# Seven block products in place of eight for 18 of the 22 input tiles of a last projection

## The chip, the cores and the metric

The kernel runs on one core of a Trainium2 chip. A core has a matrix engine (TensorE, PE in the profile), three engines for elementwise work (VectorE or DVE, ScalarE or ACT, GpSimd or POOL), a queue engine (SyncE, SP) that issues most transfers, and 16 DMA engines. The on-chip memory SBUF and the accumulators PSUM (eight banks of 128 x 512 floats) have 128 partitions; HBM is the memory outside. The metric is the time of one execution on the device in microseconds. Of several runs the median is given.

## The reference

One layer of a diffusion backbone over 512 latent tokens of width 1024, with 256 context tokens: a token mixer, then a gated MLP with a 3x3 depthwise convolution on its gate branch, and a final RMSNorm. The change lies in the second half:

```python
h = modulate(rms_norm(x_lat, norm2_g), sh2, sc2)
x_lat = x_lat + gt2 * conv_ffn(h, w_up, conv_w, conv_b, w_down)
return rms_norm(x_lat, final_g)

def conv_ffn(h, w_up, conv_w, conv_b, w_down, rows, cols):
    val, gate = jnp.split(h @ w_up, 2, axis=-1)
    gate = depthwise_conv_grid(gate, conv_w, conv_b, rows, cols)
    return (jax.nn.gelu(gate, approximate=False) * val) @ w_down
```

The inner width is 2816, that is 22 tiles of 128 channels. `x_lat` at this point, after the token mixer, is called x2 in the kernel.

## The kernel before

**Products.** Every product is made in three matmuls (`mm3`): both factors are split into a high part (a cast to the fp32r type, by ScalarE) and a low part (the difference, a subtraction by GpSimd or, where the call says `V`, by VectorE), and high x high, high x low and low x high are added up in PSUM. `split` is that pair of operations; `split_w` does it for a 128 x 1024 weight tile, into a ring of four pairs (`whl`, tags whi and wlo). Weight tiles arrive through a ring of three raw tiles (`raw_tile`). A further ring, `S4`, has 30 tiles of 128 x 1024 for everything that lives longer.

**Up projection.** It runs over the 22 channel tiles. For tile i, `up_weights` loads two weight tiles (gate and value), `up_mm` makes 48 matmuls into two PSUM banks (tag pb, four banks, so two tiles of them), and `up_out` finishes: ScalarE starts the convolution with the middle tap, VectorE adds the other eight taps, reading PSUM, ScalarE applies the Gelu, VectorE multiplies by the value branch, and `split` by ScalarE and VectorE leaves the tile of hidden values (128 channels x 512 tokens, high and low) in `hid[i]`, one S4 tile. The first three tiles overlap the norm before them. In four of the tiles (4, 8, 12, 16) VectorE also works out a quarter of the gate vector gt2 (`mod_part`, with two loads of 512 KB), which `mod_bcast` adds to the broadcast tile `gt2` one tile later.

**Last projection.** The hidden tiles are the stationary factor, in blocks of 128 tokens, and `w_down`'s rows the moving one, 512 columns at a time. All of the output, four token blocks by two halves, stands in the eight PSUM banks (`acc`). For each of the first 18 input tiles, `load_down` loads 512 KB of w_down, VectorE multiplies it by gt2, `split_w` splits it with ScalarE and GpSimd, and `down` makes 4 x 2 x 3 = 24 matmuls. The last NL = 4 input tiles are loaded and split ahead (`wl_`, in S4 tiles) and are done block by block of tokens at the end, so that one block's residual add, norm and store run beside the products of the next. x2 stands in four SBUF tiles (pool emf) from the norm to the end.

**Order.** The program is written as one sequence; a planner orders each engine's instructions by a simulated timeline, with the sequence as priority, and places buffers from the free ones of a ring. `tc.issue_after(x)` holds an instruction back until x is issued. Each engine then runs its own list in order. SP issues almost all loads in such a list, and waits in it for buffers to come free.

Helpers that record most operations have one line each, so nearly all groups of the profile carry L88 or L87, and tiles tell them apart: ac is the convolution, raw a loaded weight tile, whi and wlo its parts, s any S4 tile, pb and p the PSUM tiles of one and two banks, x the tiles of x2.

Of the kernel before, what the change touches and what calls it, by code (L numbers as in the profile page):

```python
# [9 lines left out]
F32 = mybir.dt.float32  # L10
# [3 lines left out]
ALU = mybir.AluOpType  # L14
# [7 lines left out]
GH = 4  # L22
FF = 2816
NF = FF // 128
EPS = 1e-6
ATT_SCALE = 96.0 ** -0.5
GQ_SCALE = 128.0 ** -0.5
# [43 lines left out]
def block_kernel(ctx: ExitStack, tc: tile.TileContext, p, out):  # L71
# [43 lines left out]
    def S4(shape, dt=F32R):  # L115
        return tl(s4, shape, dt, "s4")
# [16 lines left out]
    def tt(eng, out_, a, b, op):  # L133
        return eng.tensor_tensor(out=out_, in0=a, in1=b, op=op)
# [153 lines left out]
    def mp_tile():  # L288
        return sm(256, "mp", 2)
# [1032 lines left out]
    behind.clear()  # L1322


    emf = ctx.enter_context(tc.tile_pool(name="emf", bufs=1))
# [23 lines left out]
    with tc.tile_pool(name="emg", bufs=1) as em_:  # L1349
# [52 lines left out]
        def w_out_norm(t):  # L1402
            cs = slice(t * 128, (t + 1) * 128)
            mp = p2()
            for k in range(8):
                for half in range(2):
                    hs = slice(half * 512, (half + 1) * 512)
                    mm3(mp[:, hs], mg[k][:, 0, cs], mg[k][:, 1, cs], wo[k][0][:, hs], wo[k][1][:, hs], k == 0, k == 7)
            xn = mraw()
            for half in range(2):  # L1410
                hs = slice(half * 512, (half + 1) * 512)
                tt(V, xn[:, hs], mp[:, hs], gt1[:, hs], ALU.mult)
                tt(V, x2[t][:, hs], x2[t][:, hs], xn[:, hs], ALU.add)
# [43 lines left out]
            up_mm(w0[i], ps0[i], 256, 512)  # L1457


    with tc.tile_pool(name="eff", bufs=1) as ef:  # L1460
        fg = tl(ef, [128, 1024], F32, "fg")
        gt2 = tl(ef, [128, 1024], F32, "gt2")
        G.dma_start(out=gt2, in_=p["b_ada"][0:1, 5120:6144].broadcast_to([128, 1024]))
        G.dma_start(out=fg, in_=p["final_g"].rearrange("(a b) -> a b", a=1).broadcast_to([128, 1024]))
        hid, gelu = [], []

        def up_out(i, ps):
            gp, vp = ps
            ac = tl(ef, [128, 512], F32, "ac", 2)

            def cw(dy, dx):
                n = ((dy + 1) * 3 + dx + 1) * NF + i
                return cwT[:, n:n + 1]

            A.activation(ac, gp, AF.Identity, scale=cw(0, 0), bias=col("conv_b", i))
            g3 = gp.rearrange("p (r c) -> p r c", c=64)
            a3 = ac.rearrange("p (r c) -> p r c", c=64)
# [12 lines left out]
            hid.append(hd)  # L1490

        for i in range(3):
            up_out(i, ps0[i])
        for i in range(3, NF):
            w = up_weights(i)
            if i in (4, 8, 12, 16):
                part = mod_part(5120 + (i - 4) * 64, mp_tile(), raw_tile)
            ps = (pb(), pb())
            up_mm(w, ps, 0, 512)
            up_out(i, ps)  # L1500

            if i in (5, 9, 13, 17):
                mod_bcast(part, gt2[:, (i - 5) * 64:(i - 1) * 64])

        acc = []
        for t in range(4):
            if t < 2:
                z = p2()
                acc.append([z[:, 0:512], z[:, 512:1024]])
            else:  # L1510
                acc.append([pb(), pb()])

        def down(k, t, half, w, a=0, n=512):
            cs, hs = slice(t * 128, (t + 1) * 128), slice(half * 512 + a, half * 512 + a + n)
            mm3(acc[t][half][:, a:a + n], hid[k][:, 0, cs], hid[k][:, 1, cs], w[0][:, hs], w[1][:, hs], k == 0,
                k == NF - 1)

        def load_down(k):

            r = raw_tile()  # L1520
            SY.dma_start(out=r, in_=w_down[:, k, :])
            tt(V, r, r, gt2, ALU.mult)
            return r

        NL = 4
# [3 lines left out]
        for k in range(NF - NL):  # L1529
            if k in (8, 10, 12, 14):  # L1530
                r = load_down(NF - NL + k // 2 - 4)
                wl_.append((S4([128, 1024]), S4([128, 1024])))
                split(*wl_[-1], r)
            w = split_w(load_down(k))
            for t in range(4):
                for half in range(2):
                    down(k, t, half, w)

        def residual(t, a, b, ps):
            tt(V, x2[t][:, a:b], x2[t][:, a:b], ps, ALU.add)  # L1540

        for t in range(4):
            last = t == 3
            o_t = tl(ef, [128, 1024], F32, "ot", 2)
# [76 lines left out]
```

## Time and profile before

| | |
|---|---|
| median of 3 runs | 895.43 us (895.09 to 897.04) |
| profiled execution | 894.83 us, its span 893.0 us |
| granted TensorE clock | 0.999 |
| HBM read, written | 97.78 MB, 2.10 MB |
| busy in the span: POOL | 372.5 us |
| loads of w_down | 22 of 512 KB, 3.6 us each to landing |

The span goes from the first to the last instruction. A line of the profile's groups gives line, engine, operation, output and inputs, shape, count, busy time, mean of one in ns, and the idle time in front of it with what ended it. A line of the chain gives start, length, and the work that the end of the kernel waited for then. Matmuls overlap one another, so the length of a chain piece divided by its matmuls, not the duration of a single one, is the time that each takes.

### The profile page before, as it was taken

Reading aid. Unit: us, or ns where it says so; the run is one execution under the profiler, and the core shown is the slowest. Engines: PE = TensorE matmul, PEld = TensorE weight load, DVE = VectorE, ACT = ScalarE, POOL = GpSimd, SP = SyncE. Lnnn points to the kernel's source line nnn. Section 1 sums busy time; section 2 is a strip of 40 time slices with the busy share of each in tenths; the row PEclk is TensorE's granted clock in tenths of the full one; section 3 lists DMA queues with packets and bytes.
Section 4 is the critical chain, followed back from the end, with each engine's and each line's share of the span. In section 5 each row is a group of like instructions: output and inputs, shape, how many; then the busy total and the mean of one; then the engine's idle time right before and its main releaser. Section 6 shows DMA issues by size and latency. Waiting matters only on the chain.

```text
span 893.0 us, 12644 instructions
## 1 busy us (share of the span) xinstructions
PE 878.4 (98%) x4852; PEld 748.1 (84%) x4852; DVE 608.2 (68%) x993; ACT 391.8 (44%) x648; POOL 372.5 (42%) x221
## 2 busy tenths in 40 slices
PE   7999999999999999999999999999999999999996
PEld 5788899888888888888888899888888888888885
DVE  5487788876978686845763775987778778744404
ACT  4365676763463636334554332443333333322204
POOL 2512364460624343433754324344444444356704
PEclk9999999999999999999999999999999999999999
DMA  9960001225414241437963314425343433244202
GB/s 293 319 175 1 1 5 33 72 72 165 106 48 134 52 135 51 119 89 249 274 209 95 95 48 138 122 72 143 96 139 110 131 114 95 70 142 142 71 0 95
DMA packets 131564, 100.89 MB, mean 113 GB/s; under 512 B 6826, under 2 KB 121874, under 8 KB 131504
## 3 DMA queue, kind: packets, MB, share of 16 engines
q1 hardware_dynamic: 130560, 98.09, 37.6%
q0 software_dynamic: 688, 1.70, 0.5%
q8 instruction: 38, 0.62, 0.3%
q10 hardware_dynamic: 256, 0.30, 0.1%
q14 instruction: 22, 0.18, 0.1%
HBM read 97.78 MB, written 2.10 MB: 112 GB/s over the span
## 4 chain that ended last, share of the span: by engine, by line
PE 92%; DVE 3%; DMA 2%; ACT 2%; issue 1%; POOL 0%; SPq 0%; DVEq 0%; ACTq 0%; POOLq 0%
PE pb L88 49%; PE p L88 23%; PE pb L87 14%; PE p L87 6%; DMA raw<-in_w_ada_dram 2%; DVE s L88 1%; ACT P L88 1%; DVE mx L88 0%; DVE kT L88 0%; ACT ph L88 0%; DVE P L88 0%; ACT kT L88 0%; ACT s L88 0%; DVE X L88 0%; DVE pl L88 0%
## 5 line engine op out<-in xcount | busy, mean ns | idle before, releaser
L88 POOL TENSOR_TENSOR wlo<-raw,whi 128x1024 fp32r<-128x1024 f32 (+1 forms) x106 | 242.8, 2298 | 322.1 <-ACT whi L88 291.5
L88 PE MATMUL pb<-s,whi 128*128 128x512 f32 (+1 forms) x906 | 272.2, 383 | 0.0
L88 PEld LDWEIGHTS pb<-s,whi 128*128 128x128 f32 x906 | 167.4, 188 | 32.1
L88 PE MATMUL pb<-s,wlo 128*128 128x512 f32 (+1 forms) x453 | 172.9, 382 | 0.0
L88 ACT CAST whi<-raw 128x1024 fp32r<-128x1024 f32 (+1 forms) x106 | 103.1, 975 | 142.3 <-issue 60.1
L88 DVE SCALAR_TENSOR_TENSOR ac<-pb,cwT,ac 128x441 f32<-128x441 f32 (+2 forms) x160 | 110.8, 693 | 12.3 <-ACT ac L88 8.6
L87 PE MATMUL pb<-s,whi 128*128 128x512 f32 x320 | 101.2, 394 | 0.0
L88 PEld LDWEIGHTS pb<-s,wlo 128*128 128x128 f32 x453 | 85.2, 188 | 16.4
L88 PE MATMUL p<-s,s 128*128 128x512 f32 (+1 forms) x392 | 81.9, 364 | 0.6 <-DVE s L88 0.5
L88 PEld LDWEIGHTS p<-s,s 128*128 128x128 f32 x392 | 65.9, 189 | 12.5 <-DVE s L88 1.1
L88 PE MATMUL p<-whi,s 128*128 128x512 f32 x208 | 69.2, 393 | 0.0
L87 PEld LDWEIGHTS pb<-s,whi 128*128 128x128 f32 x320 | 59.3, 188 | 11.5
L88 DVE TENSOR_TENSOR raw<-raw,gt 128x1024 f32<-128x1024 f32 x22 | 39.2, 1783 | 35.6 <-DMA raw<-in_w_down_dram 35.6
L87 PE MATMUL pb<-s,wlo 128*128 128x512 f32 x160 | 62.8, 393 | 0.0
L88 PE MATMUL pb<-whi,s 128*128 128x512 f32 x176 | 57.7, 390 | 0.0
L88 ACT ACTIVATE ac<-ac 128x512 f32<-128x512 f32 x22 | 13.9, 632 | 80.0 <-DVE ac L88 80.0
L88 PEld LDWEIGHTS p<-whi,s 128*128 128x128 f32 x208 | 39.1, 188 | 8.2 <-ACT s L88 0.3
L88 POOL TENSOR_TENSOR s<-raw,s 128x1024 fp32r<-128x1024 f32 (+1 forms) x10 | 24.5, 2461 | 43.2 <-ACT s L88 43.2
L88 PE MATMUL pb<-s,s 128*32 128x128 f32 (+2 forms) x322 | 41.4, 315 | 0.9 <-DMA s<-in_w_ada_dram 0.9
L88 PE MATMUL p<-kT,s 128*128 128x512 f32 (+1 forms) x192 | 41.2, 351 | 0.9 <-ACT P L88 0.9
L88 DVE TENSOR_TENSOR pl<-pb,ph 128x512 fp32r<-128x512 f32 x48 | 32.9, 686 | 13.0 <-ACT ph L88 12.5
L88 PE MATMUL p<-wlo,s 128*128 128x512 f32 x104 | 40.5, 390 | 0.0
(252 smaller groups left out, 1554.4 us busy)
## 6 DMA issues: line engine op xcount, KB each, us to landing
raw<-in_w_up_dram SPq DMA_DIRECT2D x44, 512.0 KB, 3.9
raw<-in_w_in_dram SPq DMA_DIRECT2D x28, 512.0 KB, 4.1
raw<-in_w_down_dram SPq DMA_DIRECT2D x22, 512.0 KB, 3.6
s<-in_w_ada_dram SPq DMA_DIRECT2D x20, 512.0 KB, 6.3
raw<-in_w_ada_dram SPq DMA_DIRECT2D x18, 512.0 KB, 4.4
xn<-in_w_ada_dram SPq DMA_DIRECT2D x10, 512.0 KB, 4.9
kT<-in_w_in_dram SPq DMA_DIRECT2D x8, 320.0 KB, 7.7
s<-in_x_dram SPq DMA_DIRECT2D x4, 512.0 KB, 5.0
```

The source lines that it names most:

```text
L87: return fn(*args, **kw)
L88: ins = fn(*args, **kw)
```

## The change

Channel tiles are taken in pairs (NP = 9 pairs, tiles 0 to 17). Tokens are halved (256 each) and output columns are halved (512 each), so that a pair is a product of 2 x 2 blocks: A11, A12 (first token half; even and odd tile), A21, A22 (second half), times B11, B12 (columns of the even tile's rows of w_down) and B21, B22 (of the odd tile's). Eight block products become seven (Winograd's form), with sums of the factors: S1 = A21 + A22, S2 = S1 - A11, S3 = A11 - A21, S4 = A12 - S2; T1 = B12 - B11, T2 = B22 - T1, T3 = B22 - B12, T4 = B21 - T2. The sum over the nine pairs is made in PSUM for each of the seven products, and the products are combined once.

- `up_out` for tiles below 18 writes A-blocks and their sums to `edge` (A11, S1, S3, S2, A21) and `second` (A12, S4, A22) by VectorE; `edge`'s first four are split into the S4 tiles `first`, `second` is kept unsplit.
- `weight_sums(n)`, in up tiles 6, 8, ..., 20 and 21, loads the pair's two tiles of w_down into a ring of two (`rawd`), VectorE makes T1 and T3, GpSimd T2 and T4, and SP stores both tiles to HBM (`sums_`).
- In the last projection a first loop over the pairs makes the four products p1 = A11 B11, p6 = S2 T2, p7 = S3 T3, p5 = S1 T1 in all eight banks, with weights from w_down and from `sums_`; they are combined into u1, u2, u7, c22 in SBUF; a second loop makes p2 = A12 B21, p4 = A22 T4, p3 = S4 B22. Their splits are by VectorE.
- The weights of these 18 tiles aren't multiplied by gt2 any more; `gated` multiplies the combined output by it and adds x2. The last four tiles stay as they were, with PSUM begun afresh.
- x2 is stored to HBM by ACT's queue after the norm and loaded again in the last projection; its SBUF goes to `second` and gt2. gt2's and final_g's loads move from POOL's queue to SP's. The parts of gt2 are made in tiles 6, 10, 14, 18. The descriptor scratch of DMAs issued by GpSimd is 4096 bytes.
- One add of 256 columns goes from the last token block.

```diff
+NP = (NF - NL) // 2
+SUM_AT = [6, 8, 10, 12, 14, 16, 18, 20, 21]
...
+    x2_ = [tl(hbm, [128, 1024], F32, f"x2_{t}") for t in range(4)]
+    sums_ = [tl(hbm, [128, 2048], F32, f"ws_{i}") for i in range(NP)]
...
             A.activation(xn, x2[t], AF.Square, accum_out=s2)
+            A.dma_start(out=x2_[t], in_=x2[t])
             r2 = rstd_exp(s2, 1, 1.0 / D)
...
+    emf_.__exit__(None, None, None)
+    kept = ctx.enter_context(tc.tile_pool(name="kept", bufs=1))
+    gt2 = tl(kept, [128, 1024], F32, "gt2")
+    SY.dma_start(out=gt2, in_=p["b_ada"][0:1, 5120:6144].broadcast_to([128, 1024]))
...
-            tt(V, ac, vp, ac, ALU.mult)
-            hd = S4([128, 2, 512])
-            split(hd[:, 0, :], hd[:, 1, :], ac, V)
-            hid.append(hd)
+            if i >= 2 * NP:
+                tt(V, ac, vp, ac, ALU.mult)
+                hid[i] = S4([128, 2, 512])
+                split(hid[i][:, 0, :], hid[i][:, 1, :], ac, V)
+            elif i % 2 == 0:
+                edge[0] = tl(ef, [128, 1280], F32, "edge", 1)
+                z = grp(edge[0], 5)
+                tt(V, z[:, 0::4, :], grp(vp, 2), grp(ac, 2), ALU.mult)
+                sub(V, z[:, 2, :], z[:, 0, :], z[:, 4, :])
+            else:
+                z = grp(edge[0], 5)
+                second.append(tl(kept, [128, 768], F32, "second", NP))
+                q = grp(second[-1], 3)
+                tt(V, q[:, 0::2, :], grp(vp, 2), grp(ac, 2), ALU.mult)
+                tt(V, z[:, 1, :], z[:, 4, :], q[:, 2, :], ALU.add)
+                sub(V, z[:, 3, :], z[:, 1, :], z[:, 0, :])
+                sub(V, q[:, 1, :], q[:, 0, :], z[:, 3, :])
+                first.append((S4([128, 1024]), S4([128, 1024])))
+                split(*first[-1], edge[0][:, 0:1024], V if i > 1 else G)
+
+        def weight_sums(n):
+
+            r = [tl(ef, [128, 1024], F32, "rawd", 2) for _ in range(2)]
+            for i in range(2):
+                SY.dma_start(out=r[i], in_=w_down[:, 2 * n + i, :])
+            b11, b12, b21, b22 = [z[:, x:x + 512] for z in r for x in (0, 512)]
+            sub(V, b11, b12, b11)
+            sub(V, b12, b22, b12)
+            sub(G, b22, b22, b11)
+            sub(G, b21, b21, b22)
+            return r
...
+            if i in SUM_AT:
+                n = SUM_AT.index(i)
+                with tc.issue_after(load[0].ins):
+                    for k, r in enumerate(weight_sums(n)):
+                        SY.dma_start(out=sums_[n][:, k * 1024:k * 1024 + 1024], in_=r)
...
+        def product(ps, hl, c, w, b, start, stop):
+            for t in range(2):
+                cs, bs = slice(c + t * 128, c + t * 128 + 128), slice(b, b + 512)
+                mm3(ps[t], hl[0][:, cs], hl[1][:, cs], w[0][:, bs], w[1][:, bs], start, stop)
...
+        p1, p6, p7, p5 = halves(p2()), halves(p2()), [pb(), pb()], [pb(), pb()]
...
+        for n in range(NP):
+            r = raw_()
+            SY.dma_start(out=r[:, 0:512], in_=w_down[:, 2 * n, 0:512])
+            SY.dma_start(out=r[:, 512:1024], in_=sums_[n][:, 1536:2048])
+            wa = split_w(r, eng=V)
+            r = raw_()
+            SY.dma_start(out=r, in_=sums_[n][:, 0:1024])
+            wb = split_w(r, eng=V)
+            a, z = n == 0, n == NP - 1
+            product(p1, first[n], 0, wa, 0, a, z)
+            product(p6, first[n], 768, wa, 512, a, z)
+            product(p7, first[n], 512, wb, 512, a, z)
+            product(p5, first[n], 256, wb, 0, a, z)
...
+        for t in range(2):
+            A.copy(u1[t], p1[t])
+        for t in range(2):
+            tt(V, u2[t], p6[t], u1[t], ALU.add)
+        for t in range(2):
+            tt(V, u7[t], p7[t], u2[t], ALU.add)
+        for t in range(2):
+            tt(V, c22[t], p5[t], u7[t], ALU.add)
+            tt(V, u2[t], p5[t], u2[t], ALU.add)
+        p2_, p4, p3 = halves(p2()), [pb(), pb()], [pb(), pb()]
...
+        x2 = [S4f() for _ in range(4)]
+        for t in (2, 3, 0, 1):
+            SY.dma_start(out=x2[t], in_=x2_[t])
...
+        for n in range(NP):
+            if n:
+                bw.append(back_weights(n))
+            if n < NP - 2:
+                back(n, (2, 4, 3), bw[n])
+        for x in (2, 4, 3):
+            for n in (NP - 2, NP - 1):
+                back(n, (x,), bw[n])
+
+        def gated(t, half, src, plus):
+
+            hs = slice(512 * half, 512 * half + 512)
+            if src is not None:
+                tt(V, plus, src, plus, ALU.add)
+            tt(V, plus, plus, gt2[:, hs], ALU.mult)
+            tt(V, x2[t][:, hs], x2[t][:, hs], plus, ALU.add)
...
-                    residual(t, 768, 1024, acc[t][1][:, 256:512])
```

`raw_` takes three of five tiles from the raw ring and two from `rawd`. `back_weights(n)` loads and splits the odd tile of w_down (1024 columns), T4 of two pairs at a time (512 each), and `second[n]` (768); for pair 0 it runs during pair 6 of the first loop, into S4 tiles. The four kept weight tiles (`wl_`) are loaded in pairs 2, 4, 6 and 8 of the first loop.

More of the change, by code (lines that the diff above doesn't have):

```diff
@@ L1495, in block_kernel @@
             w = up_weights(i)
[L1496 to L1497 removed]
+            if i in (6, 10, 14, 18):
+                part = mod_part(5120 + (i - 6) * 64, mp_tile(), raw_tile)
             ps = (pb(), pb())
@@ L1523, in load_down, with back_raw, back_hl, back_weights @@
             return r
-        NL = 4
+        t4 = [None]
+        def back_raw(n):
+            return raw_() if n else S4f()
+        def back_hl(n):
+            return whl() if n else (S4([128, 1024]), S4([128, 1024]))
+        def back_weights(n):
+            r = back_raw(n)
+            SY.dma_start(out=r, in_=w_down[:, 2 * n + 1, :])
+            w = back_hl(n)
+            split(*w, r, V)
+            if n % 2 == 0:
+                k = min(2, NP - n)
+                r = back_raw(n)
+                for i in range(k):
+                    SY.dma_start(out=r[:, 512 * i:512 * i + 512], in_=sums_[n + i][:, 1024:1536])
+                h_, l_ = back_hl(n)
+                split(h_[:, 0:512 * k], l_[:, 0:512 * k], r[:, 0:512 * k], V)
+                t4[0] = h_, l_
+            h_, l_ = S4([128, 768]), S4([128, 768])
+            split(h_, l_, second[n], V)
+            return w, t4[0], (h_, l_)
+        bw = []
+        p1, p6, p7, p5 = halves(p2()), halves(p2()), [pb(), pb()], [pb(), pb()]
         wl_ = []
@@ L1532, in block_kernel @@
                 wl_.append((S4([128, 1024]), S4([128, 1024])))
                 split(*wl_[-1], r)
[L1534 to L1537, printed above, removed]
+            if n == NP - 3:
+                bw.append(back_weights(0))
+        u1, u2, u7, c22 = halves(S4f()), halves(S4f()), halves(S4f()), halves(S4f())
+        for t in range(2):
+            A.copy(u1[t], p1[t])
+        for t in range(2):
+            tt(V, u2[t], p6[t], u1[t], ALU.add)
@@ new lines, in block_kernel, with back @@
+        for t in range(2):
[4 more added lines that the diff above has]
+        p2_, p4, p3 = halves(p2()), [pb(), pb()], [pb(), pb()]
+        def back(n, which, w):
+            z = n == NP - 1
+            for x in which:
+                if x == 2:
+                    product(p2_, w[2], 0, w[0], 0, n == 0, z)
+                elif x == 4:
+                    product(p4, w[2], 512, w[1], n % 2 * 512, n == 0, z)
+                else:
+                    product(p3, w[2], 256, w[0], 512, n == 0, z)
@@ new lines, in block_kernel, with down @@
+        for t in range(2):
+            gated(2 + t, 1, None, c22[t])
+        for t in range(2):
+            gated(t, 0, p2_[t], u1[t])
+        for t in range(2):
+            gated(2 + t, 0, p4[t], u7[t])
+        for t in range(2):
+            gated(t, 1, p3[t], u2[t])
+        acc = []
+        for t in range(4):
+            acc.append(halves(p2()) if t < 2 else [pb(), pb()])
+        def down(k, t, half, w, a=0, n=512):
+            cs, hs = slice(t * 128, (t + 1) * 128), slice(half * 512 + a, half * 512 + a + n)
+            mm3(acc[t][half][:, a:a + n], hid[k][:, 0, cs], hid[k][:, 1, cs], w[0][:, hs], w[1][:, hs], k == NF - NL,
+                k == NF - 1)
```

44 lines of the change are left out of this document (19 added, 25 removed).

## The prediction

> **What bounds the kernel now.** I read the page's summary first, then the chain of work that ended last in order of time, then the busy time by stretches, then single instructions of VectorE (DVE) and GpSimd (POOL) in the up projection.
>
> ```profile
> span 893.0 us, 12644 instructions
> PE 878.4 (98%) x4852; PEld 748.1 (84%) x4852; DVE 608.2 (68%) x993; ACT 391.8 (44%) x648; POOL 372.5 (42%) x221
> PE 92%; DVE 3%; DMA 2%; ACT 2%; issue 1%; POOL 0%; SPq 0%; DVEq 0%; ACTq 0%; POOLq 0%
> ```
>
> TensorE is busy in 98% of the span and makes 92% of the chain, so an instruction taken from it shortens the kernel unless something else ends later. The changed stages in the chain (start, length, count of matmuls):
>
> ```profile
> 559.96 206.35 PE pb L88 x910
> 766.30 2.72 PE p L88 x12
> ...
> 861.50 2.72 PE pb L88 x12
> 864.22 10.88 PE p L88 x48
> 875.10 11.04 PE pb L88 x60
> 886.15 0.02 issue
> ```
>
> The up projection ends at 766.30, the first 18 input tiles of the last projection at 864.22, the four left for the end at 886.15. No other engine stands in these rows: PE never waited. From 766.30 to 864.22 are 97.92 us for 18 x 24 = 432 matmuls of 512 columns: 0.2267 us each. The up projection's 910 in 206.35 us give the same, 48 matmuls or 10.88 us per tile.
>
> The other engines, by stretches (length, PE, PEld, DVE, ACT, POOL busy, clock, DMA share, GB/s). Three of these hold four up tiles each, one with part of the gt2 vector; before them is the start of the up tiles, behind them the last projection:
>
> ```profile
> 560.00:590.00 30.00, 30.00 (x134) 24.85 (x133) 27.99 (x46) 14.54 (x20) 12.09 (x5) 1.00 0.37 108
> 597.26:641.43 44.17, 44.17 (x196) 36.59 (x195) 33.97 (x50) 15.89 (x21) 19.38 (x9) 1.00 0.41 119
> 641.43:685.20 43.77, 43.77 (x194) 36.27 (x193) 34.64 (x50) 15.20 (x20) 18.95 (x8) 1.00 0.42 121
> 685.20:729.00 43.80, 43.80 (x195) 36.29 (x194) 34.30 (x49) 15.16 (x21) 19.18 (x8) 1.00 0.42 120
> 777.00:820.00 43.00, 43.00 (x191) 35.64 (x190) 16.58 (x10) 12.22 (x12) 28.54 (x12) 1.00 0.37 123
> ```
>
> PE is full in all. In the up projection DVE is next, 34.3 of 43.8 us; in the last projection DVE has 16.6 of 43.0 and the DMA engines a third. Work added to the up projection falls on the engine with the least room.
>
> **What PE loses.** A pair of input tiles takes 2 x 24 = 48 matmuls now, and seven products x 2 token blocks x 3 = 42 after, of the same shape. Nine pairs: 54 matmuls less, 54 x 0.2267 = **12.24 us**. The four tiles at the end keep their 96. That is the whole gain, since nothing else in the changed stages is on the chain; all that follows is what may be given back. The profiled execution took 894.83 us, 1.83 more than its span and 0.60 less than the median of 895.43. So 894.83 - 12.24 = 882.59, and on the level of the median 883.2 if nothing stalls.
>
> **What the up projection gains: DVE.** The rows that carry it:
>
> ```profile
> 530.16 1.42 DVE L88 TENSOR_TENSOR s<-ht,s 128x256 fp32r<-128x256 f32 x4
> 611.42 1.72 DVE L88 TENSOR_TENSOR s<-ac,s 128x512 fp32r<-128x512 f32 x1
> 653.27 0.69 DVE L88 TENSOR_TENSOR ac<-pb,ac 128x512 f32<-128x512 f32 x1 [0.37 <-ACT ac L88]
> 654.73 2.48 DVE L88 TENSOR_TENSOR s<-ac,s 128x512 fp32r<-128x512 f32 x1 [0.76 <-ACT s L88]
> 665.13 0.69 DVE L88 TENSOR_TENSOR s<-ac,s 128x512 fp32r<-128x512 f32 x1 [0.76 <-ACT s L88]
> 666.69 5.81 DVE L88 SCALAR_TENSOR_TENSOR ac<-pb,cwT,ac 128x441 f32<-128x441 f32 x8 [0.86 <-ACT ac L88]
> 698.99 2.47 DVE L88 TENSOR_TENSOR s<-ac,s 128x512 fp32r<-128x512 f32 x1 [0.77 <-ACT s L88]
> 759.20 1.22 DVE L88 TENSOR_TENSOR raw<-raw,gt 128x1024 f32<-128x1024 f32 x1 [0.35 <-DMA raw<-in_w_down_dram]
> L88 DVE TENSOR_TENSOR s<-ac,s 128x512 fp32r<-128x512 f32 x12 | 12.9, 1076 | 7.8 <-ACT s L88 7.8
> 654.26 2.40 POOL L88 TENSOR_TENSOR wlo<-raw,whi 128x1024 fp32r<-128x1024 f32 x1 [5.19 <-ACT whi L88]
> 666.06 4.77 POOL L88 TENSOR_TENSOR wlo<-raw,whi 128x1024 fp32r<-128x1024 f32 x2 [6.12 <-ACT whi L88]
> L88 POOL TENSOR_TENSOR x<-x,fg 128x512 f32<-128x512 f32 x7 | 9.1, 1311 | 31.1 <-ACT ot L88 31.1
> ```
>
> The multiply ac<-pb,ac stays, with its output moved. Per four tiles (two pairs) the change takes away four subtractions s<-ac,s, 4 x 1.076 = 4.3 us as measured. It adds eight sums of 256 columns (8 x 0.355 = 2.8), two subtractions of 1024 (2 x 1.22 = 2.4) and four of 512 on the weights (4 x 0.69 = 2.8): 8.0 us. So 34.3 - 4.3 + 8.0 = 38.0 us, before any wait for POOL.
>
> That wait is real. The subtraction at 654.73 took 2.48 us where its twin at 665.13 took 0.69: a POOL subtraction ran from 654.26 to 656.66, and DVE ended 0.55 us after it. The eight taps at 666.69, which read PSUM, kept their 5.81 us beside two POOL operations. The twelve of the group (12.9 us) lost it in three places, 1.72, 2.48 and 2.47 us; the other nine took 0.69. The mean loss is 1.076 - 0.69 = 0.39 us. All the new operations read SBUF twice, and POOL gets four more of 1.31 us per four tiles: 19.2 + 5.2 = 24.4 of 43.8, 56% busy.
>
> The Trainium skill, "SBUF — State Buffer", section "Who interferes with whom", says that a DVE instruction with two SBUF inputs and a GpSimd instruction that reads SBUF exclude each other: the second to issue blocks for the whole of the first. The 2.48 us row agrees. The rule speaks against this change; what it would make of the time is the third rival.
>
> The new operations come in groups (the one difference, the three sums of the odd tile, its subtraction, the two on weights), two of each per four tiles: 8 groups. Bounds: no wait, 38.0; 0.39 for each of the 14 operations, 43.5; each group meeting POOL in 56% of cases and then losing 1.79 us (2.48 - 0.69), 38.0 + 8.0 = 46.0. I take 0.39 per group, the row's own mean, since operations that follow one another wait once: 38.0 + 3.1 = 41.1. DVE can be that busy only if the gaps left by ACT fill up. With a backlog it reached 27.99 of 30.00 us, 93%, with no stall of PE, that is 40.9 of 43.8 us. So 0.2 us is lacking per four tiles, over 16 tiles (6 to 21) some **1 us**; with the bounds 0, 10 and 20. PE does not feel it at once: two tiles' pairs of PSUM banks lie between them.
>
> **What else the up projection gains.** ACT has the same columns to cast, 15 of 44 us busy. It is charged nothing. POOL's 56% delays the low halves of up weights, which are made a tile ahead, more than 10 us early; I cost it at nothing, and if that cover goes PE waits the 2.4 us of a POOL operation. DMA: two loads and two stores of 512 KB per pair, 2.1 MB in 21.8 us, 96 GB/s beside 120. At 0.42 busy for 120, the four more take about 0.3: 0.7, no bound. On SP's queue the two stores wait for POOL's last sum, and the w_up loads behind them wait too; three raw tiles and the tile of lead cover it. If not, a load comes late by one such wait, about 3 us.
>
> The issue of x2's stores goes to ACT's queue, between the square and the two activations of the norm.
>
> ```profile
> L88 ACTq DMA_DIRECT2D out_dram<-x x1: 381/381/381, 889.2 to 889.2; - x1
> 526.63 0.75 DVE L88 TENSOR_SCALAR xn<-x,rr 128x1024 f32<-128x1024 f32 x1
> 533.60 1.04 PE L88 MATMUL pb<-cst,xn 128*128 128x128 f32 x8
> ```
>
> 0.38 us, while the last norm is ready at 527.4 and PE reads it at 533.6: 6 us of cover, so nothing. gt2's load now waits for these stores on SP; it is first used at tile 7.
>
> **From the up to the last projection.** Four banks come free as DVE finishes tiles 20 and 21.
>
> ```profile
> 763.20 0.69 DVE L88 TENSOR_TENSOR ac<-pb,ac 128x512 f32<-128x512 f32 x1 [0.76 <-ACT ac L88]
> 775.06 0.69 DVE L88 TENSOR_TENSOR ac<-pb,ac 128x512 f32<-128x512 f32 x1 [0.76 <-ACT ac L88]
> ```
>
> The second frees the banks that p5 takes, 9.5 us after PE's last up matmul. In front of p5 PE has p1, p6 and p7 of two pairs (36 matmuls, 8.2 us) and p1, p6 of the third (2.7 us): 10.9 us. DVE loses the multiplies by gt2 that stand between the taps here and gets the splits of these weights, 1.22 us each either way. I take no stall; a DVE three us later costs 1.6.
>
> **First half (p1, p6, p7, p5), 24 matmuls, 5.44 us per pair.** DVE two splits, 2.4 us, and half a multiply by gt2; ACT two casts of 1.05 us:
>
> ```profile
> L88 ACT CAST whi<-raw 128x1024 fp32r<-128x1024 f32 x24 | 25.2, 1050 | 23.1 <-issue 18.0 <-POOL wlo L88 4.7 <-PE pb L88 0.5
> ```
>
> Both stay under 5.44. DMA moves 1.05 MB per pair; with the four kept tiles and the first weights of the second half 12.6 MB in 49 us, 276 GB/s from pair 2 on. The loads of w_down ran at 123 GB/s with 0.37 busy, which is 332 GB/s at full; the up weights' at 119 with 0.41, 290. Rows half as long, which some of the new loads have, lie between, by my choice. So 83 to 95% in the worst stretch: it holds, with little to spare.
>
> **Between the halves.** p2 waits for two ACT copies, with 4 us of p6, p7 and p5 over them; p4's banks are free when p5 ends. p3 needs two sums for C22 and the first u2, 3 x 0.69 = 2.1 us after p5, under 2.7 us of p2 and p4; one split ahead of them costs 0.6. The second pair's `second` needs tiles that the last `first` frees: cast, split, behind 2.8 us of sums, 4.4 us against 4.08, 0.4. The four loads of x2 and fg (2.6 MB, 7.9 us at 332 GB/s) fall in with the next weights: I take 1 of it. Together **2 us**, bounds 0 and 8. Then 18 matmuls, 4.08 us per pair, over 2.8 us of DVE (2304 columns) and 236 GB/s: no bound.
>
> **End.** Of the last 12 operations with x2, 8 us of DVE, 2.7 us are over p3's last products and the rest over the first four-tile block of 5.44 us; the chain behind 886.15 keeps its instructions.
>
> **Sum.** 883.2 + 1 + 2 = **886.2**.
>
> **Rivals.** (1) *DMA bursts.* The queue behind x2 and the late half-width loads is not drained in time: the 8 us bound instead of 2, 883.2 + 1 + 8 = 892. For: 276 of 290 to 332 GB/s, and SP blocks in order. Against: PE now never waits for w_down, and the five raw tiles run ahead. Chance 0.08. (2) *The gain is eaten by the up projection*, 0.39 us for each operation: 883.2 + 10 + 2 = 895, no change. Chance 0.08. (3) *Slower: the lock between DVE and POOL makes DVE the bound of the up projection.* With 46.0 us needed and 40.9 to be had, 5.1 us per four tiles, 20 us over 16: 883.2 + 20 + 2 = 905. It decides from 14 us of stalls, where DVE's need passes 44 us per four tiles. For: the 2.48 us row. Against: in nine of twelve tiles the same subtraction took 0.69, and the taps, most of DVE's work, run beside POOL. The rule of the Trainium skill named above says the same of every such meeting, and leaves open how often they meet. Chance 0.10. (4) *It does not save what it says*, if a product's matmuls took longer than 0.2267: shapes and types are the same, 0.02, near no change.
>
> **How the numbers follow.** The forecast (stalls of 0 to 7 us, 883 to 890) has 0.72. Faster: 0.72 + 0.08 = 0.80; within 0.2% (893.6 to 897.2, about what a measurement of this kernel can tell from no change): 0.08 + 0.02 = 0.10; slower 0.10. The range goes from 883.0, no stall at all, to 893.6, and so leaves out (2), (3) and (4).
>
> **What would show it.** Right: in the chain the last projection's first 18 tiles take 378 matmuls and about 86 us, with up to 2 us of gaps where p4 and p3 begin; up tiles stay at 10.88 us; DVE at 40 to 42 of 43.8. Wrong: PE waiting for ac or for DVE between tiles 6 and 21 (rivals 2, 3), DVE subtractions of 128x512 well over 1.08 us; PE waiting for whi or wlo in the last projection with SP or DMA behind them (rival 1).

## The result, and the profile after

| | before | after |
|---|---|---|
| median of 4 runs each | 895.52 us (895.09 to 897.04) | 926.11 us (923.97 to 928.02) |
| span of the profiled execution | 893.0 us | 924.7 us |
| first matmul of the last projection | 766.14 us | 805.94 us |
| PE busy from there to the end | 119.99 us, 541 matmuls | 108.76 us, 487 matmuls |

After / before is 1.0338, 95% interval 1.0312 to 1.0364: slower by 3.4%, where 1% faster was forecast. Executions of one kernel, the kernel before included, differ by some 4 us for a cause that was not followed up, so each ratio is to several runs of the kernel before, on the same chip. The table already says where. The last projection got shorter, about as foreseen; the up projection, whose matmuls of full width start at about 557.6 us in both, got 39.8 us longer. In the page of the changed kernel, span, busy times and the chain's shares are:

```profile
span 924.7 us, 12841 instructions
PE 875.9 (95%) x4798; PEld 740.7 (80%) x4798; DVE 703.1 (76%) x1089; ACT 409.6 (44%) x664; POOL 354.5 (38%) x220
...
PE 63%; DVE 17%; issue 7%; DMA 7%; ACT 3%; POOL 2%; SPq 0%; DVEq 0%; ACTq 0%; POOLq 0%
```

DVE now has 17% of the chain that ended last. Whom PE waits for is answered by its waits (microseconds in total, times, longest):

```profile
PE pb L91 <- DVE ac L91: 28.9, 5, 8.9
PE p L91 <- DVE s L91: 4.0, 3, 2.1
```

Where it waits, the timeline of its matmuls tells, with the idle time in front of one in brackets (four lines, from the up projection):

```profile
592.81 0.69 PE L91 MATMUL pb<-s,whi 128*128 128x512 f32 x2 [2.27 <-DVE ac L91]
...
648.29 0.76 PE L91 MATMUL pb<-s,whi 128*128 128x512 f32 x1 [8.75 <-DVE ac L91]
...
703.92 0.77 PE L91 MATMUL pb<-s,whi 128*128 128x512 f32 x1 [8.90 <-DVE ac L91]
...
758.67 0.76 PE L91 MATMUL pb<-s,whi 128*128 128x512 f32 x1 [7.99 <-DVE ac L91]
```

PE waits for the convolution `ac`: for VectorE to give PSUM banks back. With three short gaps (1.03, 0.69 and 0.67 us) that is 30.3 us. The four lines lie four up tiles apart, so the windows between them are the profile's view by stage: length, busy time of PE, PEld, DVE, ACT and POOL, granted clock, DMA share, GB/s.

```profile
592.81:648.29 55.48, 45.02 (x195) 36.11 (x195) 50.20 (x60) 14.91 (x19) 24.95 (x12) 0.96 0.53 170
648.29:703.92 55.63, 46.73 (x194) 38.08 (x195) 50.12 (x60) 14.96 (x19) 24.92 (x12) 0.90 0.53 171
703.92:758.67 54.75, 46.76 (x194) 37.67 (x195) 50.13 (x60) 14.97 (x19) 24.92 (x12) 0.94 0.54 173
```

Four tiles take 55.3 us, where before they took 43.8. VectorE is busy for 50.15 of them, more than PE has work for. That is rival 3's picture, with a larger need than its 46.0. What VectorE does in that time is in its groups for the three windows together (12 up tiles; count | busy us, mean ns | idle before it):

```profile
L91 DVE SCALAR_TENSOR_TENSOR mp<-raw,csilu,mp 128x256 f32<-128x256 f32 x21 | 22.4, 1067 | 3.1 <-DMA raw<-in_w_ada_dram 2.9
...
L91 DVE TENSOR_TENSOR edge<-edge 128x256 f32<-128x256 f32 x12 | 17.0, 1414 | 0.3
L91 DVE TENSOR_TENSOR second<-second,edge 128x256 f32<-128x256 f32 x6 | 11.8, 1964 | 0.2
L91 DVE TENSOR_TENSOR s<-edge,s 128x1024 fp32r<-128x1024 f32 x6 | 10.0, 1671 | 0.0
L91 DVE TENSOR_SCALAR mp<-raw,csilu 128x256 f32<-128x256 f32 x3 | 7.5, 2492 | 0.0
...
L91 DVE TENSOR_TENSOR edge<-edge,second 128x256 f32<-128x256 f32 x6 | 3.7, 624 | 0.1
```

A sum of 256 columns, foreseen at 0.355 us (the pace of four in a row; a single one lasts 0.42 us undisturbed), takes 0.62 to 1.96 us on average. The `mp` steps, which make the parts of gt2 and which the change only moved to other tiles, got slower as well: in 12 tiles of the kernel before (597 to 729 us) the same 21 took 577 ns on average, here 1067. One odd tile shows why, first in VectorE's timeline (start, length, operation):

```profile
603.27 0.83 DVE L91 TENSOR_TENSOR edge<-edge,second 128x256 f32<-128x256 f32 x1
604.14 1.40 DVE L91 TENSOR_TENSOR edge<-edge 128x256 f32<-128x256 f32 x1
605.57 2.51 DVE L91 TENSOR_TENSOR second<-second,edge 128x256 f32<-128x256 f32 x1
```

and then in GpSimd's for the same stretch:

```profile
602.52 1.29 POOL L91 TENSOR_TENSOR rawd<-rawd,rawd 128x512 f32<-128x512 f32 x1 [5.78 <-DVE rawd L91]
603.89 1.36 POOL L91 TENSOR_TENSOR rawd<-rawd 128x512 f32<-128x512 f32 x1
605.21 2.58 POOL L91 TENSOR_TENSOR wlo<-raw,whi 128x1024 fp32r<-128x1024 f32 x1
```

The three VectorE sums are alike, yet took 0.83, 1.40 and 2.51 us. They ended at 604.10, 605.54 and 608.08; the three GpSimd operations ended at 603.81, 605.25 and 607.79. Each sum ended 0.29 us after a GpSimd operation, and each after another one: the next GpSimd operation had begun when the next sum came.

### The profile page after: what moved, and what is told of

Same layout as the page of the kernel before. It is cut to its first block, busy times and chain, and to the rows that moved or that the text cites. A ratio compares the mean times of both kernels' runs of the same rounds, so it can differ in the third digit from the quotient of the medians.

```text
span 924.7 us, 12841 instructions
## 1 busy us (share of the span) xinstructions
PE 875.9 (95%) x4798; PEld 740.7 (80%) x4798; DVE 703.1 (76%) x1089; ACT 409.6 (44%) x664; POOL 354.5 (38%) x220
## 4 chain that ended last, share of the span: by engine, by line
PE 63%; DVE 17%; issue 7%; DMA 7%; ACT 3%; POOL 2%; SPq 0%; DVEq 0%; ACTq 0%; POOLq 0%
PE pb L91 27%; PE p L91 17%; PE pb L90 14%; PE p L90 6%; DVE ac L91 5%; DVE mp L91 3%; DMA raw<-in_w_ada_dram 3%; DMA rawd<-in_w_down_dram 2%; DVE s L91 2%; DVE edge L91 2%; DVE second L91 1%; POOL wlo L91 1%; ACT s L91 1%; DMA raw<-in_w_down_dram 1%; DVE wlo L91 1%
## 5 line engine op out<-in xcount | busy, mean ns | idle before, releaser
L91 POOL TENSOR_TENSOR wlo<-raw,whi 128x1024 fp32r<-128x1024 f32 (+1 forms) x88 | 196.4, 2242 | 283.8 <-ACT whi L91 253.4
L91 PE MATMUL pb<-s,whi 128*128 128x512 f32 (+1 forms) x906 | 277.4, 389 | 29.3 <-DVE ac L91 27.9
L91 PEld LDWEIGHTS pb<-s,whi 128*128 128x128 f32 x906 | 169.8, 192 | 65.9 <-issue 31.2
L91 PE MATMUL p<-s,s 128*128 128x512 f32 (+1 forms) x398 | 84.5, 364 | 2.1 <-DVE s L91 2.0
L90 PEld LDWEIGHTS pb<-s,whi 128*128 128x128 f32 x320 | 59.3, 188 | 11.5
L91 PE MATMUL p<-whi,s 128*128 128x512 f32 x168 | 56.2, 393 | 0.0
L91 PE MATMUL pb<-whi,s 128*128 128x512 f32 x164 | 53.7, 390 | 0.0
L91 PE MATMUL pb<-s,s 128*32 128x128 f32 (+2 forms) x340 | 46.3, 319 | 0.9 <-DMA s<-in_w_ada_dram 0.9
L91 PEld LDWEIGHTS pb<-s,s 128*128 128x128 f32 (+1 forms) x340 | 36.1, 159 | 6.7 <-DVE rv L91 1.2
L91 DVE SCALAR_TENSOR_TENSOR mp<-raw,csilu,mp 128x256 f32<-128x256 f32 x35 | 35.0, 1001 | 6.4 <-DMA raw<-in_w_ada_dram 6.0
L91 PE MATMUL p<-s,whi 128*128 128x256 f32 (+1 forms) x156 | 38.6, 338 | 0.0
```

The lines of the kernel that those rows point to most:

```text
L90: return fn(*args, **kw)
L91: ins = fn(*args, **kw)
```

## The experiments

**The theories.** *The lock*: a VectorE operation that reads SBUF twice stands still while a GpSimd operation runs, and successive ones each meet a fresh GpSimd operation, so that VectorE becomes the bound. *Plain work*: the new sums take so long by themselves. *Queue or DMA*: the loads and stores of the weight sums hold up SP's queue or the memory. A fourth theory came with the second set, *the coupling*: GpSimd's two weight sums wait for VectorE's two, so that GpSimd runs just when VectorE goes on to its own sums, and that alone makes most meetings.

**The measure.** The time lost to the lock is counted like this: for each group of VectorE operations that read SBUF, its count times the excess of its mean over the same form undisturbed. The undisturbed durations come from the experiments: 0.425 us for 256 columns, 0.69 for 512, 1.22 for 1024, 0.48 for a gt2 step and 0.35 for the first of its chain. From the rows above: 12 x 0.989 + 6 x 1.539 + 6 x 0.45 + 6 x 0.2 + 21 x 0.587 + 3 x 2.14 = 43.7 us in 12 tiles, **14.6 us per four tiles**; of this 8.3 on the new operations and 6.2 on the gt2 steps. Before, it was 3.6, with 2.1 on the gt2 steps. In the table each kernel's own groups over the same 12 tiles give its sum, and the time of four tiles is a third of that between matmuls of PE at the same place twelve tiles apart (e6: (737.73 - 594.20) / 3 = 47.8).

All experiments, each an edit of the changed kernel; the ratio is to the kernel before, run on the same chip:

| run | edit | median us (runs) | ratio, 95% interval | four up tiles us | lock us per four |
|---|---|---|---|---|---|
| before | | 895.52 (4) | | 43.8 | 3.6 |
| after | | 926.11 (4) | 1.0338 (1.0312 to 1.0364) | 55.3 | 14.6 |
| e1 | no weight sums at all | 894.32 (8) | 0.9970 (0.9952 to 0.9989) | 44.8 | 6.4 |
| e2 | weight sums' arithmetic out | 893.11 (8) | 0.9953 (0.9933 to 0.9972) | 45.0 | 4.5 |
| e3 | data sums in PSUM | 905.75 (3) | 1.0095 (1.0062 to 1.0128) | 47.8 | 5.4 |
| e4 | e3, gt2 steps in PSUM too | 894.11 (10) | 0.9963 (0.9942 to 0.9984) | 43.8 | 0.1 |
| e5 | gt2 steps alone in PSUM | 914.03 (2) | 1.0187 (1.0152 to 1.0221) | 50.0 | 8.7 |
| e6 | all weight sums on VectorE | 910.88 (2) | 1.0165 (1.0134 to 1.0196) | 47.8 | 6.7 |
| e8 | all weight sums on GpSimd | 912.85 (2) | 1.0174 (1.0139 to 1.0209) | 50.2 | 12.0 |
| e9 | e4, weight sums two tiles earlier | 890.29 (5) | 0.9923 (0.9894 to 0.9952) | | |
| e10 | e9, all weight sums on GpSimd | 888.24 (4) | 0.9898 (0.9863 to 0.9933) | | |
| e12 | e10, last four tiles' splits on VectorE | 884.54 (6) | 0.9877 (0.9853 to 0.9900) | PE without a gap | |

The kernel before had medians of 897.22 beside e1 to e4, 896.97 beside e5 and e8 to e10, and 895.53 beside e6 and e12.

### e1 and e2: without the weight sums

e1 leaves the stage out:

```diff
-            if i in SUM_AT:
-                n = SUM_AT.index(i)
-                with tc.issue_after(load[0].ins):
-                    for k, r in enumerate(weight_sums(n)):
-                        SY.dma_start(out=sums_[n][:, k * 1024:k * 1024 + 1024], in_=r)
...
-            SY.dma_start(out=r[:, 512:1024], in_=sums_[n][:, 1536:2048])
+            SY.dma_start(out=r[:, 512:1024], in_=w_down[:, 2 * n, 512:1024])
...
-            SY.dma_start(out=r, in_=sums_[n][:, 0:1024])
+            SY.dma_start(out=r, in_=w_down[:, 2 * n + 1, :])
```

(and in `back_weights` likewise).

> Left out: weight_sums (its loads, its four subtractions, its stores); the last projection reads the same number of bytes from w_down instead of the kept sums. Lock theory (VectorE and GpSimd block each other, and that makes VectorE the bound of the up projection): VectorE loses 2.8 us of its own per four up tiles and some 4 us of waits behind GpSimd's two 1.3 us sums, so four tiles take about 49 us in place of 55.6, still over 43.8, and the kernel about 902 to 908 us. Queue theory (SP's queue and the DMA engines, loaded with the sums' loads and stores, bring up weights and the parts of gt2 late): four tiles are back at 43.8 to 45, the kernel at 886 to 890.

e2 keeps loads, stores and waits, without the four subtractions:

```diff
             b11, b12, b21, b22 = [z[:, x:x + 512] for z in r for x in (0, 512)]
-            sub(V, b11, b12, b11)
-            sub(V, b12, b22, b12)
-            sub(G, b22, b22, b11)
-            sub(G, b21, b21, b22)
             return r
```

> Left out: the four subtractions of weight_sums; its loads and stores stay, and w_down's own values are kept. Lock theory: as without the sums altogether, within 3 us of that run. Queue theory: the loads and stores are the cost, so four up tiles stay at 53 to 56 us and the kernel over 918.

894.32 and 893.11 us. The queue theory falls: with every load and store of the weight sums in place, e2 has lost all of the 31 us. (e1 alone would not have told: its four tiles came out as the queue theory had them, its time between the two.) The lock theory stands in kind, but its 902 to 908 was too slow: to take away 2.8 us of VectorE's work and 5.2 us of GpSimd's took away 8 to 10 us of waiting as well. The groups of e2 from 593 to 730 us, a little over 12 up tiles, show which:

```profile
L91 DVE TENSOR_TENSOR edge<-edge 128x256 f32<-128x256 f32 x13 | 13.3, 1026 | 0.4
...
L91 DVE TENSOR_TENSOR edge<-edge,second 128x256 f32<-128x256 f32 x6 | 2.5, 425 | 0.2
L91 DVE TENSOR_TENSOR second<-second,edge 128x256 f32<-128x256 f32 x6 | 2.5, 425 | 0.2
```

Two of the four sums of a pair, 1964 and 624 ns before, are undisturbed at 425; the other two, at 1026 ns, still meet the split of up weights by GpSimd. The gt2 steps fall from 1067 to 572 ns (in e1 only to 1004). But the shorter time would come from plain work too: both runs also took work away. The next two keep it.

### e3 and e4: the same operations, one operand in PSUM

e3 writes the data sums into two PSUM banks that stand idle in the up projection. An operation was given at most one input from PSUM, so ScalarE copies A11 to SBUF:

```diff
-                edge[0] = tl(ef, [128, 1280], F32, "edge", 1)
-                z = grp(edge[0], 5)
-                tt(V, z[:, 0::4, :], grp(vp, 2), grp(ac, 2), ALU.mult)
-                sub(V, z[:, 2, :], z[:, 0, :], z[:, 4, :])
+                edge[0] = tl(ef, [128, 1024], F32, "edge", 1) if i == 0 else p2()
+                z, z0 = grp(edge[0], 4), tl(ef, [128, 256], F32, "z0", 1)
+                tt(V, z[:, 0:2, :], grp(vp, 2), grp(ac, 2), ALU.mult)
+                A.copy(z0, z[:, 0, :])
+                sub(V, z[:, 2, :], z0, z[:, 1, :])
...
-                tt(V, z[:, 1, :], z[:, 4, :], q[:, 2, :], ALU.add)
-                sub(V, z[:, 3, :], z[:, 1, :], z[:, 0, :])
+                tt(V, z[:, 1, :], z[:, 1, :], q[:, 2, :], ALU.add)
+                sub(V, z[:, 3, :], z[:, 1, :], z0)
...
-                split(*first[-1], edge[0][:, 0:1024], V if i > 1 else G)
+                split(*first[-1], edge[0], V if i > 1 else G)
```

> The data sums of pairs 1 to 8 stand in PSUM (A11, A21 then S1, S3, S2 in two banks, with a copy of A11 in SBUF made by ScalarE), so that each of these sums and the subtraction of the split reads SBUF once. Same count and sizes on VectorE. Lock theory: by the groups of the changed kernel these operations lost (1492-415)x13 + (1964-415)x6 + (624-415)x6 + (1671-1215)x6 ns = 27 us in three groups of four tiles, 9 each; four tiles take 46 to 48 us, the kernel 890 to 898. Theory of plain work (VectorE has too many instructions, the waits are only slack): no change, over 920. Queue theory: no change, over 918.

e4 also lets the gt2 steps add up in PSUM:

```diff
-                part = mod_part(5120 + (i - 6) * 64, mp_tile(), raw_tile)
+                ap_ = mod_part(5120 + (i - 6) * 64, p2()[:, 0:256], raw_tile)
+                part = mp_tile()
+                A.copy(part, ap_)
```

> As the run with the data sums in PSUM, and the running sum of gt2's parts in PSUM too (ScalarE copies it to SBUF for the broadcast). Lock theory: the gt2 steps lost 6.9 us per four tiles more; VectorE's need falls to about 36 of 43.8 us, TensorE sets the pace again, four tiles 43.8 to 44.5, the kernel 885 to 889, faster than before. Plain work and queue theories: no change, over 918.

905.75 and 894.11 us. VectorE does as many operations as in the changed kernel, on the same columns, with GpSimd's work untouched; only the place of operands differs (and ScalarE's copies come on top), and e4 is faster than the changed kernel by 32 us. Plain work falls. The groups of e4 over 595 to 730 us:

```profile
L91 DVE SCALAR_TENSOR_TENSOR p<-raw,csilu,p 128x256 f32<-128x256 f32 x25 | 12.0, 480 | 0.1
L91 DVE TENSOR_TENSOR s<-p,s 128x1024 fp32r<-128x1024 f32 x6 | 7.3, 1213 | 0.0
...
L91 DVE TENSOR_TENSOR p<-p,second 128x256 f32<-128x256 f32 x6 | 2.6, 432 | 0.2
L91 DVE TENSOR_TENSOR p<-p,z 128x256 f32<-128x256 f32 x6 | 2.6, 430 | 0.1
L91 DVE TENSOR_TENSOR second<-second,p 128x256 f32<-128x256 f32 x6 | 2.5, 421 | 0.2
L91 DVE TENSOR_TENSOR p<-z,p 128x256 f32<-128x256 f32 x6 | 2.5, 420 | 0.0
```

Their waits are gone: 420 to 432 ns for the sums, 480 for a gt2 step. This agrees with the Trainium skill, "SBUF — State Buffer", section "Who interferes with whom", which says that a VectorE instruction with at most one SBUF input, outside the 2-port modes, does not contend with GpSimd. A second input is not all that matters here: the first step of a gt2 chain (`mp<-raw,csilu`) reads one SBUF tile, and it took 2492 ns in the changed kernel, 341 in e6, and 477 in e4, where it writes to PSUM. No run shows in which mode it ran.

e3 kept its forecast for four tiles (47.8 us; the waits fell by 9.2) and missed that for the kernel, 890 to 898 us, which would take four such savings. They came in the twelve tiles only, 143.3 us in place of 165.9; the four behind them took 46.7 in place of 47.3. In the twelve, the gt2 steps, still in SBUF, keep most of their waits, 5.4 us per four tiles in place of 6.2:

```profile
L91 DVE SCALAR_TENSOR_TENSOR mp<-raw,csilu,mp 128x256 f32<-128x256 f32 x21 | 25.1, 1195 | 2.1 <-DMA raw<-in_w_ada_dram 2.0
...
L91 DVE TENSOR_TENSOR rawd<-rawd 128x512 f32<-128x512 f32 x6 | 4.2, 693 | 8.2 <-DMA rawd<-in_w_down_dram 8.2
...
L91 DVE TENSOR_SCALAR mp<-raw,csilu 128x256 f32<-128x256 f32 x3 | 2.1, 705 | 0.0
```

The steps that add up wait longer than in the changed kernel (1195 ns in place of 1067), the first ones of a chain less (705 in place of 2492). VectorE also stands 8.2 us for the loads of w_down.

e4 missed its 885 to 889 us. It is PE-bound in the up projection up to 748 us, but has one gap later, where the last weight sums crowd, and behind it the granted clock was 0.50 until about 757 us:

```profile
751.38 0.79 PE L91 MATMUL pb<-s,whi 128*128 128x512 f32 x1 [2.92 <-DVE ac L91]
```

### e5: the gt2 steps alone

Only the second diff of e4.

> Only the running sum of gt2's parts stands in PSUM; the data sums read SBUF twice again, as in the changed kernel. Lock theory: the gt2 steps lost (1067-480)x21 + (2492-480)x3 ns = 18.4 us in three groups of four tiles, 6.1 each; four tiles take about 49.5 us in place of 55.6, the kernel 900 to 908 us. Plain work: no change, over 920.

914.03 us, more than expected. The gt2 steps are at 483 ns, but the data sums keep their waits (`edge<-edge` 1278 ns, `second<-second,edge` 1964, the split 2052), 8.7 us per four tiles. Each of the two edits alone wins less than its forecast had, but they add up: e3 wins 20 us, e5 12, both together 32, and then PE is the bound for most of the up projection.

### e6 and e8: the weight sums on one engine

```diff
-            sub(G, b22, b22, b11)
-            sub(G, b21, b21, b22)
+            sub(V, b22, b22, b11)
+            sub(V, b21, b21, b22)
```

> All four weight sums by VectorE, as the only edit to the changed kernel: VectorE gets 2.8 us more of its own work per four up tiles, GpSimd loses its 5.2 us there. Plain work (VectorE has too many instructions): four tiles go from 55.3 to about 58 us, the kernel to 935 us or more. Lock theory: what counts is how long VectorE stands behind GpSimd; the waits fall from 14.6 to 7 to 10 us per four tiles, so four tiles take 50 to 54 us and the kernel 905 to 920, less than the changed kernel in spite of the added work.

910.88 us. e6 gives VectorE 2.8 us per four tiles *more* work than the changed kernel (4 x 0.69) and takes 5.2 from GpSimd, and it is 15 us faster; its waits (6.7 us) and its four tiles (47.8 us) came out under the forecast. So VectorE's amount of work is not what set 926; how often it meets GpSimd is.

e8 is the opposite, `V` to `G` in the first two subtractions.

> All four weight sums by GpSimd, as the only edit to the changed kernel; VectorE loses 2.8 us per four up tiles and no engine waits for VectorE's half of them, GpSimd gains 5.2 us. Lock theory: the data sums and gt2 steps now wait behind twice as many GpSimd sums; four tiles stay at 51 to 56 us, the kernel 912 to 926. Coupling theory (what costs is that GpSimd stands in its queue for VectorE's half, 28.5 us in the up projection, with up weights' low halves and SP's stores and loads behind it): GpSimd runs freely, four tiles take 44 to 47 us, the kernel under 900.

912.85 us. VectorE has 2.8 us less of work and GpSimd 5.2 more, and nothing couples the two. The coupling theory, under 900, falls: the other operations still meet GpSimd's sums. But four tiles took 50.2 us, a little less than the lock theory's 51 to 56, and the waits did not grow with the added sums, they fell from 14.6 to 12.0 us. How much of the meetings the coupling makes is not separated.

### e9, e10 and e12: towards a kernel that beats both

e9 is e4 with the weight sums two tiles earlier:

```diff
-SUM_AT = [6, 8, 10, 12, 14, 16, 18, 20, 21]
+SUM_AT = [4, 6, 8, 10, 12, 14, 16, 18, 20]
```

> Data sums and gt2's running sum in PSUM, as in the run with both, and the weight sums made in tiles 4, 6, ..., 20 in place of 6, ..., 20, 21, so that the last pair is not loaded, summed and stored in the same tile as the first weights of the last projection. Lock theory with the stall of that run explained by the crowded end (TensorE waited 2.9 us at 751 us and ran slower after it): no stall left in the up projection, 5 us less than the run with both, ratio to before 0.989 to 0.992. If the stall had another cause: the ratio stays at 0.996.

890.29 us: the 2.92 us gap at 751 is gone (0.8 and 0.7 us of PE's waits are left from 590 to 760). The ratio, 0.9923, is just above the forecast, and its interval overlaps e4's a little.

e10 adds e8's edit, since GpSimd's sums should now disturb nobody.

> As the run with the earlier weight sums, and all four of them by GpSimd, so that VectorE never waits for a load of w_down in the up projection (it waited 12.5 us in twelve tiles of the run with both in PSUM, hidden under TensorE). Lock theory: VectorE reads nothing twice from SBUF in the paired tiles, so GpSimd's extra 5.2 us per four tiles delay nobody; ratio 0.988 to 0.992. Rival: GpSimd, some 30 of 44 us busy, brings the low halves of up weights late, TensorE waits for wlo, ratio over 0.995.

888.24 us, ratio 0.9898: as the lock theory has it, PE has no gap in the up projection. e12 also gives the splits of the last four tiles' weights to VectorE:

```diff
-                split(*wl_[-1], r)
+                split(*wl_[-1], r, V)
```

> As the run with the earlier weight sums by GpSimd and both running sums in PSUM, and the splits of the four kept weight tiles by VectorE in place of GpSimd, so that nothing blocks VectorE in the last projection (there single subtractions of 1.2 us took 2.7 to 3.7). Lock theory: the stall of 1.5 us where p2 begins shrinks, 1 to 2 us less than that run, ratio to before 0.986 to 0.990. Rival: the joint waits for other things (banks, loads), same time as that run, ratio 0.990.

884.54 us, 0.9877 of the kernel before: the fastest that was run. PE's gaps in the last projection, 0.95 and 1.53 us in e10, are gone. By their times e9, e10 and e12 are not told apart with certainty, their intervals overlap. In e12's windows in the up projection PE has no gap and the full clock, although GpSimd is busy for 30.5 of 45 us (the last of the five busy times; before, 19.4 of 44.2):

```profile
595.00:640.00 45.00, 45.00 (x200) 37.27 (x199) 36.90 (x62) 17.94 (x24) 30.59 (x17) 1.00 0.71 226
640.00:685.00 45.00, 45.00 (x201) 37.23 (x200) 34.16 (x56) 16.83 (x22) 30.40 (x17) 1.00 0.68 219
```

## Why the prediction was wrong

**The matmuls saved: right.** 54 fewer, at 0.2267 us each 12.24 us. The windows from the first matmul of the last projection to the end have in their second number PE's busy time. In the kernel before:

```profile
766.14:893.00 126.86, 119.99 (x541) 99.75 (x539) 51.17 (x59) 32.30 (x51) 60.08 (x27) 0.99 0.26 87
```

In e12:

```profile
768.89:884.60 115.71, 107.76 (x487) 89.53 (x485) 85.22 (x114) 53.37 (x76) 12.12 (x7) 0.99 0.48 164
```

119.99 - 107.76 = 12.23. In the changed kernel itself it was 119.99 - 108.76 = 11.23 of PE's busy time, and from the first matmul to PE's last end, with 2.2 us of gaps at the joints, 119.99 - 110.9 = 9.1.

**The joints of the last projection: right in size, by luck.** 2 us foreseen, 2.17 measured (0.28, 0.40 and 1.49). But half of the 2 us stood for loads, which caused no gap. The longest gap is in front of products that go into banks which the first sums read, and those sums came late since a split by VectorE ahead of them took 3.00 us in place of 1.22, beside GpSimd's split of a kept weight tile:

```profile
859.26 0.50 PE L91 MATMUL p<-s,s 128*128 128x512 f32 x1 [1.49 <-DVE s L91]
```

```profile
853.87 3.00 DVE L91 TENSOR_TENSOR wlo<-raw,whi 128x1024 fp32r<-128x1024 f32 x1 [0.34 <-ACT whi L91]
```

```profile
852.98 2.82 POOL L91 TENSOR_TENSOR s<-raw,s 128x1024 fp32r<-128x1024 f32 x1 [12.40 <-ACT s L91]
```

e12, where VectorE makes that split itself, has no such gap.

**DMA bursts (rival 1): did not come.** No gap of PE in the last projection ends on a DMA, though the share rose from 0.26 to 0.47 or 0.48.

**The up projection: the failed step.** VectorE's need was forecast as 38.0 us for its work and 3.1 for the lock, per four tiles, "since operations that follow one another wait once". The work was right: 50.15 - 14.6 = 35.6 us undisturbed, with the 2.1 us of waiting on the gt2 steps that the 38.0 contained 37.7. The lock was not: 14.6 - 2.1 = 12.5 us in place of 3.1. Two things were wrong in it.

- Operations that follow one another do *not* wait once. The rows at 603 to 608 us show three that waited for three. As long as GpSimd has work at hand, it starts the next operation while VectorE's is ending. This brought the new operations to 8.3 us, above the highest bound (8.0), which had counted one meeting per group.
- Operations that the change did not make were left out. The gt2 steps read SBUF twice as well, and their waiting rose from 2.1 to 6.2 us per four tiles. Without weight sums on GpSimd it is 3.7 (e1), 1.9 (e2) and 1.5 us (e6), so GpSimd's 5.2 us of added work are behind much of the rise; e1 shows that they are not all of it. In the kernel before, over 12 tiles, these steps were:

```profile
L88 DVE SCALAR_TENSOR_TENSOR mp<-raw,csilu,mp 128x256 f32<-128x256 f32 x21 | 12.1, 577 | 3.1 <-DMA raw<-in_w_ada_dram 2.9
...
L88 DVE TENSOR_SCALAR mp<-raw,csilu 128x256 f32<-128x256 f32 x3 | 5.2, 1730 | 2.1 <-DMA raw<-in_w_ada_dram 2.0
```

With 50.15 in place of 41.1, the prediction's own step, need against 40.9 to be had, over 16 tiles, gives 37 us; 39.8 came, though spread otherwise: 34.5 in the twelve tiles (165.86 - 131.4), 3.8 in the last four (47.27 in place of 43.50). The mechanism was rival 3's, with its place right and its price (20 us) too low by half. Its chance of 0.10 rested on "in nine of twelve tiles the same subtraction took 0.69". That counts how often one lone operation a tile meets GpSimd; it says nothing about several in a row.

**What stays open.** The gaps sum to 30.3 of 39.8 us. Most of the rest is slower matmuls: in the three windows PE is busy 138.5 us for 12 tiles' products that took 3 x 43.8 = 131.4 before, at clocks of 0.90 to 0.96. Where VectorE is the bound, slower matmuls can also fill time that would else be a gap; how much they add by themselves no run separates.

## What to carry to other kernels

Before elementwise work is put on VectorE, list on both engines which operations read SBUF twice, the old ones of other stages too, and count for each a whole operation of GpSimd as a bound; one operand in PSUM took that waiting to zero here, where moving the work between the two engines only halved the loss. A group whose mean is far above its shortest member is no price for a run of such operations: read the timeline of both engines side by side. An algorithm that saves matmuls is worth its saving only if the engine that prepares its operands keeps slack after these waits.

## What was not expected of the hardware

**The waits chain.** A 0.42 us sum that came while GpSimd was at work ended 0.29 us after the GpSimd operation, and the next one waited for the next: 0.83, 1.40, 2.51 us. GpSimd lost little by it: its 1024-column subtraction took 2471 ns on average in the changed kernel and 2409 in e12, where VectorE's sums took PSUM operands.

**The clock after a gap.** The windows after the 8.75 us gap (the granted clock is the third number from the end):

```profile
648.30:650.00 1.70, 1.70 (x4) 1.41 (x5) 1.53 (x3) 1.50 (x2) 0.12 (x1) 0.50 0.52 151
650.00:652.00 2.00, 2.00 (x6) 1.52 (x6) 2.00 (x2) 0.00 (x0) 2.00 (x1) 0.50 1.17 321
652.00:654.00 2.00, 2.00 (x7) 1.56 (x6) 1.93 (x4) 0.00 (x0) 0.24 (x1) 0.60 1.09 341
654.00:656.00 2.00, 2.00 (x10) 1.64 (x9) 1.93 (x3) 0.00 (x0) 0.00 (x0) 1.00 1.03 373
```

Half rate until some 5.3 us after the gap. After the 2.27 us gap at 592.81 the clock was 1.00 at once. The Trainium skill, "TensorE: Matmul & The Clock Gate", part "The HAM clock gate", states half rate after an idle window of about 3.4 us. These two gaps agree with it, and no part of the prediction had priced it. But a gap shorter than that is not safe: in e8 one of 1.88 us was followed by half rate (first line), while in e5 one of 2.95 us was not (second line).

```profile
592.46:594.00 1.54, 1.54 (x4) 1.25 (x5) 1.54 (x4) 1.51 (x2) 0.00 (x0) 0.52 0.06 16
```

```profile
641.69:643.00 1.31, 1.31 (x6) 1.09 (x7) 0.00 (x0) 1.31 (x3) 0.61 (x1) 1.00 0.60 178
```

The clock record of these traces offers a reading. Its pieces of half rate inside the kernels last 3.41, 6.83 or 10.24 us, as if the rate could change only at steps of 3.41 us. From 500 us on, a step at full rate was followed by half rate when PE had been idle for 1.88 us of it or more, and by full rate up to 1.83 us (one step with 1.90 us was an exception). A gap that is cut by the end of a step, as the 2.95 us were (1.63 and 1.32), then does no harm. No run was made to test this.
